# A first product over six accumulators, and no VectorE conditioning tile inside the recurrence

## The chip, the cores and the metric

The program runs on one core of a Trainium2 chip. The metric is the device time of one execution in microseconds. A core has TensorE (PE; its weight loads are PEld), VectorE (DVE), ScalarE (ACT), GpSimd (POOL) and SyncE (SP), which here only issues DMAs. Each engine works through its own queue strictly in order and waits there for what its next instruction needs.

## The reference

A decoder trunk of four layers over 256 tokens of 1024 features, float32. Each layer has a token mixer and a gated feed-forward part with a causal convolution, and both are modulated by a conditioning vector:

```
c_act = silu(c)
for i in range(4):
    sh1, sc1, g1, sh2, sc2, g2 = split(c_act @ ada_w[i] + ada_b[i], 6)      # 1024 x 6144 per layer
    h = rmsnorm(x, mix_norm_g[i]) * (1 + sc1) + sh1
    y = (gmlp, latent attention, hgrn2, gmlp)[i](h)
    x = x + (1 + g1) * y
    h = rmsnorm(x, ffn_norm_g[i]) * (1 + sc2) + sh2
    x = x + (1 + g2) * conv_ffn(h)                                          # 1024 -> 2 x 2816 -> 1024
return rmsnorm(x, final_g)
```

The gMLP mixer computes `u, v = split(gelu(h @ w_in))` with 2048 features each, normalises v over its features, mixes it over tokens, multiplies by u and projects back. The hgrn2 mixer computes q, a forget gate f, i and g from h (1024 features each), runs a gated recurrence over the tokens, normalises, gates with silu(g) and projects back.

## The kernel before

Every weight matrix comes from HBM once. A *unit* is one raw tile of 128 x 2048 float32 (1 MiB), loaded by SP into a ring of five raw buffers. Each of its halves (128 x 1024) is split into a high part by an ACT cast (`wh`, line 215) and a low part by a DVE subtraction (`wl`, line 223); a few low parts come from an ACT multiplication and an accumulating DMA of POOL instead (lines 220 and 221). There are seven `wh` and seven `wl` buffers. A product is three matmul passes: high by high, high by low, low by high. `unit()` loads and converts up to three units ahead of the one it returns, and then calls `pacing()`.

The conditioning vectors (`c_act @ ada_w`) are computed beside the products, 1 MiB of `ada_w` at a time, in two ways. Seven of the vectors go through TensorE (`ada_tensor`, line 337, in the two halves of the PSUM bank `adaps`). Fifteen go through VectorE (`ada_vector`): four tiles each, and each tile is one DMA (line 353) and two DVE operations of multiply and sum (line 362). The table `RATE` tells how many tiles a stage starts per unit, first for TensorE, then for VectorE. `pacing()` adds the rate to a counter at each unit, loads a tile when the counter reaches one, and runs it two units later; VectorE tiles start only while more than two units of the mixer or the feed-forward part are left. `need()` runs what is missing when a vector is used. The stages, in order: `mix` (the v product), `u`, `go` of the gMLP, `up` and `dn` of the feed-forward part; `lev` (the levels of the recurrence) and `hout` in layer 2.

The order of each engine's queue comes from a list scheduler that simulates the program in the order in which it is written, and lets an instruction go ahead where it expects it to be ready. `tc.issue_after` pins an instruction behind another on its engine.

The two places that the change touches first:

- **The first product (layer 0, `proj_tok_first` with `start`).** Its input needs the first two conditioning vectors, which come in eight pieces (`ada_first`, one DMA of 1 MiB and 32 small matmuls each, line 388). The string `FIRST` interleaves them: `a3` turns two blocks of x if 3 were even (line 495), computes the 3rd piece and modulates block 3 of the input (lines 395 to 398, 509, 516, 520); `v3` multiplies this block by its weights; `d` issues the next weight load; `p` issues late parameters. The product runs K-outermost: for each of the eight blocks, the 1024 first features of v are accumulated in four PSUM banks (`acc`, four buffers), 8 high matmuls (line 750) and 4 low ones (line 758) of 512 columns each. The other 1024 features come in two blocks of 512 by `proj_tok` (lines 253 to 255). The transposed blocks of x and the pieces' sums lie in the pool `misc`, three buffers of one bank.
- **The levels of the recurrence (layer 2, `hgrn`).** After the products for f and q, DVE multiplies q by k in four pieces (line 1181), and PE sums them (`sums`, line 1165); in the loop over m from 1 to 128, ACT takes exponentials (lines 1197 and 1202), DVE multiplies and adds (1198, 1200, 1203, 1207 to 1211), and PE forms the products of neighbouring pieces (`grams`, line 1156, and lines 1224 to 1239). Between them stand the product `hi` (lines 253 to 255, four units) and `hg` (lines 705 to 709, four units).

Of the kernel before, what the change touches and what calls it, by code (L numbers as in the profile page):

```python
# [18 lines left out]
D = 1024  # L19
S = 256  # L20
L = 4
P = 128
KC = D // P
EPS = 1e-6
NF = 22
GI = 2048
# [9 lines left out]
PIECES = [(0, 0, 512), (0, 512, 512), (1, 0, 512), (1, 512, 256), (1, 768, 256)]  # L36
WARM = 22
WARM2 = 5
FIRST = "a0 d v0 a1 a2 d v1 a3 v2 a4 d v3 a5 v4 a6 d v5 a7 v6 p v7"
DMA_AHEAD = 1  # L40
LAG = 2
OLAG = 1
# [4 lines left out]
HOLD = (3, 4)  # L47
ADA_P = [(1, 1), (1, 2), (1, 3), (1, 4), (2, 3), (2, 4), (3, 5)]
ADA_D = [(l, u) for l in range(L) for u in range(6) if (l, u) > (0, 1) and (l, u) not in ADA_P]
RATE = {("mix", 0): (0.05, 0.9), ("u", 0): (0.1, 0.85), ("go", 0): (0.35, 0.4), ("up", 0): (0.1, 0.2),  # L50
        ("dn", 0): (0.0, 0.4), ("mix", 1): (2.0, 0.0), ("up", 1): (0.0, 0.26), ("dn", 1): (0.0, 0.9),
        ("mix", 2): (0.0, 0.0), ("lev", 2): (0.5, 0.3), ("hout", 2): (0.25, 0.0), ("up", 2): (0.0, 0.2),
        ("dn", 2): (0.0, 0.75), ("mix", 3): (0.0, 0.5), ("u", 3): (0.0, 0.6), ("go", 3): (0.0, 0.55),
        ("up", 3): (0.0, 0.0), ("dn", 3): (0.0, 0.0)}
MAGIC = 12582912.0
TWO_PI = 2.0 * math.pi
# [35 lines left out]
def build(ctx, tc, A, out, stages=None):  # L92
# [23 lines left out]
    def acc(name, shape=(P, 512)):  # L116
        return pp.tile(list(shape), F32, tag="acc", name=name, bufs=4)

    def misc(name, shape=(P, 512)):
        return pp.tile(list(shape), F32, tag="misc", name=name, bufs=3)  # L120
# [50 lines left out]
    def want(aps, again=()):  # L171

        plan.extend((*a, i in again) for i, a in enumerate(aps))
# [6 lines left out]
    def dma_next():  # L180
        ap, n, _ = plan[state["dma"]]
        raw = wp.tile([P, 2048], F32, tag="raw", name=f"raw{state['dma']}", bufs=NRAW)
        state["dma"] += 1
        if state["dma"] == 1:

            nc.sync.dma_start(raw[:, :1024], ap[:, :1024])
            raw_, ap = raw[:, 1024:], ap[:, 1024:]
        else:
            raw_ = raw[:, :n]
        i = nc.sync.dma_start(raw_, ap)  # L190
        state["lastdma"] = getattr(i, "ins", i)
        raws.append((raw, n))
# [34 lines left out]
    def unit(ahead=None, more=DMA_AHEAD):  # L227
        u = state["use"]
        ahead = state["ahead"] if ahead is None else ahead
        while state["dma"] < min(len(plan), u + ahead + (more if u else 0)):  # L230
            dma_next()
        while state["conv"] < min(len(plan), u + ahead) or halves:
            conv_half()
        state["use"] += 1
        r = ready.pop(0)
        pacing()
        return r

    def pace(kind, l, left=None, tag=None):
        state["rate"] = dict(zip("pd", RATE[kind, l]))  # L240
        state["gap"] = GAPS[2 * l + (kind in ("up", "dn"))]
        if left is not None:
            state["left"] = left
        if tag is not None:
            state["tag"] = tag
# [126 lines left out]
    firsts = {}  # L372

    def ada_first(l, c):

        raw = wp.tile([P, KC, 4, 64], F32, tag="raw", name=f"adaf{c}", bufs=NRAW)
        rawf = raw[:].rearrange("p a b c -> p (a b c)")
        for o in (0, 1024) if c == 0 else ():
            nc.sync.dma_start(rawf[:, o : o + 1024], A["ada0"][l, c, :, o : o + 1024])
        if c:  # L380
            nc.sync.dma_start(rawf, A["ada0"][l, c])
        ps = misc(f"adaf{c}", (P, 64))
        with contextlib.ExitStack() as es:
            if "pe" in firsts:
                es.enter_context(tc.issue_after(firsts["pe"]))
            for kc in range(KC):
                for j in range(4):
                    i = pe.matmul(ps[32 * j : 32 * j + 32, :], crep(kc), raw[:, kc, j, :], start=kc == 0, stop=kc == KC - 1,
                                  tile_position=(0, 32 * j))
            firsts["pe"] = getattr(i, "ins", i)  # L390
        firsts[c] = ps

    def first_store(l, c):
        tr = t1(f"adaft{c}", 64)
        dve.transpose(tr[:], firsts[c][:])
        for e in range(2):
            b = 8 * e + c
            dve.tensor_tensor(mod[:, l, b : b + 1], tr[:, 32 * e : 32 * e + 1], prm[:, col("ada_b", l * 48 + b) : col("ada_b", l * 48 + b) + 1],
                              op=ALU.add)
        mod_post(l, 8 + c, 1)  # L400
# [329 lines left out]

    def proj_tok_first(name, sink, start=None):

        ps = [acc(f"{name}{i}") for i in range(4)]

        def chunk(kc):
            if kc % 2 == 0:
                firsts["w"] = unit(1, 0) if start else unit(2)
            with contextlib.ExitStack() as es:
                if start and kc < KC - 1:
                    es.enter_context(tc.issue_after(firsts["pe"]))  # L740
                w = firsts["w"][kc % 2]
                if not start:
                    if kc:
                        low(kc - 1, firsts["wp"])
                    firsts["wp"] = w
                for b in range(2):
                    s = slice(b * 512, b * 512 + 512)
                    for t in range(2):
                        for e in range(2):
                            i = pe.matmul(ps[2 * b + t][:], hh[:, kc, t * P : t * P + P], w[e][:, s], start=kc == 0 and e == 0, stop=False)  # L750
                if start or kc == KC - 1:
                    i = low(kc, w)
            firsts["pe"] = state["mm"] = getattr(i, "ins", i)

        def low(kc, w):
            for b in range(2):
                for t in range(2):
                    i = pe.matmul(ps[2 * b + t][:], hlo[:, kc, t * P : t * P + P], w[0][:, b * 512 : b * 512 + 512], start=False, stop=kc == KC - 1)
            return i

        if start:
            start(chunk)
        else:
            for kc in range(KC):
                chunk(kc)
        for i in range(4):
            sink(i // 2, i % 2, ps[i])

    hk = lambda k: hh[:, k, :]
# [1 line left out]


    def gmlp_units(j):
        want([(A["gmv"][j, i], 2048) for i in range(8)])
        want([(A["gmu"][j, i], 2048) for i in range(8)])
        want([(A["gmo"][j, i], 2048) for i in range(8)])

    def gmlp(l, j, start=None):
# [6 lines left out]

        proj_tok_first("v", sink, start)
        if start:
            pace("mix", l, 20)
        proj_tok(3, "v", sink, 2)

        nsh = sm("nsh", 2)
        ss = sm("ss", 8)
# [647 lines left out]
def pack(i):  # L1440
# [19 lines left out]
    def atk(W):  # L1460

        return np.ascontiguousarray(W.reshape(-1, 2, P, D).transpose(0, 2, 1, 3)).reshape(-1, P, 2048)
# [22 lines left out]
    r["pos"] = np.ascontiguousarray(np.broadcast_to(f["positions"], (P, S)))  # L1485
    wi = f["gm_w_in"]
    r["gmu"] = np.stack([bt(w, [rng(t * P, P) for t in range(16)], 2) for w in wi])
    r["gmv"] = np.stack([np.concatenate([atk(w[:, GI : GI + D]), at(w[:, GI + D :])]) for w in wi])
    r["gmo"] = np.stack([atk(w) for w in f["gm_w_out"]])
    r["gmg"] = f["gm_ln_g"]  # L1490
    r["gmbs"] = f["gm_b_s"].reshape(2, -1)
# [39 lines left out]
```

## Time and profile before

| | |
|---|---|
| median of 3 runs | 1361.19 us (1359.21 to 1361.55) |
| the profiled execution | 1361.2 us |
| its span, first to last instruction | 1359.5 us |
| PE busy | 1318.8 us (97%) |
| DVE busy | 1108.9 us (82%) |
| ACT busy | 798.4 us (59%) |
| mean granted TensorE clock | 0.992 of 2.4 GHz |
| read from HBM | 337.45 MB, 249 GB/s over the span |

A matmul of 512 columns starts every 0.23 us and one of 256 columns every 0.12 us where PE runs without a stop; the duration that the trace lists for one (0.39 and 0.28 us) includes its way through the array and overlaps the next. So a lost microsecond is seen in the distance of starts and in the idle time in square brackets, less well in the busy share.

### The profile page before, as it was taken

How to read it: one execution, taken by the hardware profiler on the slowest of the kernel's cores; microseconds unless marked ns; L12 is line 12 of the kernel's file. 1: busy time of each engine (PE TensorE's matmuls, PEld its weight loads, DVE VectorE, ACT ScalarE, POOL GpSimd, SP SyncE). 2: the span in 40 equal slices, each digit the busy share in tenths (PEclk: the TensorE clock that was granted, in tenths of full speed). 3: DMA queues.
4: the chain of work that ended last, by engine and by line, in shares of the span. 5: the costliest groups of instructions: out<-in, count | busy, mean ns of one | idle time of the engine just before them, and what ended most of it. 6: DMA issues, size and time to landing. Idle time of an engine off the chain costs nothing.

```text
span 1359.5 us, 25127 instructions
## 1 busy us (share of the span) xinstructions
PE 1318.8 (97%) x10197; PEld 1198.6 (88%) x10197; DVE 1108.9 (82%) x1847; ACT 798.4 (59%) x1248; POOL 38.0 (3%) x47
## 2 busy tenths in 40 slices
PE   8999999999999999999978899999999999999997
PEld 7799899997787899988876879999778998999986
DVE  5699889889775789899856877888988896888874
ACT  4664576665456576654675457666455754666652
POOL 0010000000000000000021000000001000000000
PEclk9999999999999999999999999999999999999999
DMA  9978975756976466599688384466978589455550
GB/s 379 356 260 317 377 261 181 273 204 267 403 263 203 127 226 248 180 350 396 223 253 242 127 306 159 164 254 257 338 282 321 193 322 375 142 171 182 202 197 31
DMA packets 51899, 340.15 MB, mean 250 GB/s; under 512 B 6852, under 2 KB 8004, under 8 KB 12998
## 3 DMA queue, kind: packets, MB, share of 16 engines
q1 hardware_dynamic: 48032, 326.95, 64.3%
q0 software_dynamic: 2592, 9.44, 3.8%
q10 hardware_dynamic: 1160, 2.17, 0.5%
q8 instruction: 80, 1.31, 0.4%
q14 instruction: 35, 0.29, 0.1%
HBM read 337.45 MB, written 1.08 MB: 249 GB/s over the span
## 4 chain that ended last, share of the span: by engine, by line
PE 72%; DVE 13%; DMA 6%; ACT 5%; issue 4%; SPq 0%; ACTq 0%; DVEq 0%
PE up L705 11%; PE up L706 11%; PE up L709 11%; PE dn L254 4%; PE dn L255 4%; PE dn L253 4%; DVE wl L223 3%; DVE adaw L362 2%; ACT wh L215 2%; DVE x L548 2%; DMA adaf<-ada 1%; PE v L750 1%; DMA adaw<-adad 1%; DVE gated L547 1%; PE up L693 1%
## 5 line engine op out<-in xcount | busy, mean ns | idle before, releaser
L215 ACT CAST wh<-raw 128x1024 fp32r<-128x1024 f32 x418 | 429.0, 1050 | 312.0 <-PE up L706 94.6
L223 DVE TENSOR_TENSOR wl<-raw,wh 128x1024 fp32r<-128x1024 f32 x400 | 485.5, 1229 | 96.8 <-ACT wh L215 96.3
L705 PE MATMUL up<-hh,wh 128*128 128x256 f32 x1280 | 314.3, 283 | 0.0
L706 PE MATMUL up<-hlo,wh 128*128 128x256 f32 x1280 | 314.1, 283 | 0.0
L705 PEld LDWEIGHTS up<-hh,wh 128*128 128x128 f32 x1280 | 245.7, 192 | 0.8 <-ACT y L1324 0.8
L706 PEld LDWEIGHTS up<-hlo,wh 128*128 128x128 f32 x1280 | 245.7, 192 | 0.0
L709 PE MATMUL up<-hh,wl 128*128 128x256 f32 x1280 | 179.7, 283 | 0.0
L709 PEld LDWEIGHTS up<-hh,wl 128*128 128x128 f32 x1280 | 165.1, 192 | 0.0
L362 DVE CUSTOM_DVE_ANT_0 adaw<-adaw,cbc,prm 128x1024 f32<-128x1024 f32 x120 | 151.2, 1276 | 11.6 <-DMA adaw<-adad 11.6
L254 PE MATMUL dn<-wl,gh 128*128 128x512 f32 x339 | 132.6, 391 | 1.3 <-DVE wl L223 1.3
L1324 ACT ACTIVATE y<-up,cwb 128x256 f32<-128x256 f32 x176 | 99.0, 562 | 58.6 <-DVE y L1326 58.6
L253 PE MATMUL dn<-wh,gh 128*128 128x512 f32 x339 | 130.3, 390 | 1.4 <-DVE y L1326 1.4
L255 PE MATMUL dn<-wh,gl 128*128 128x512 f32 x339 | 131.0, 389 | 0.0
L1325 DVE SCALAR_TENSOR_TENSOR y<-up,cwb,y 128x255 f32<-128x255 f32 x176 | 84.2, 478 | 29.1 <-ACT y L1324 28.4
L1326 DVE SCALAR_TENSOR_TENSOR y<-up,cwb,y 128x254 f32<-128x254 f32 x176 | 83.9, 477 | 1.4
L254 PEld LDWEIGHTS dn<-wl,gh 128*128 128x128 f32 x339 | 63.6, 188 | 16.4 <-DVE wl L223 3.4
L253 PEld LDWEIGHTS dn<-wh,gh 128*128 128x128 f32 x339 | 63.6, 188 | 14.9 <-issue 1.8
L255 PEld LDWEIGHTS dn<-wh,gl 128*128 128x128 f32 x339 | 63.6, 188 | 13.1
L705 PE MATMUL u<-hh,wh 128*128 128x256 f32 x256 | 64.6, 290 | 0.0
L706 PE MATMUL u<-hlo,wh 128*128 128x256 f32 x256 | 62.8, 283 | 0.0
L654 DVE TENSOR_TENSOR gl<-g,gh 128x256 fp32r<-128x256 f32 x88 | 37.0, 420 | 20.9 <-ACT gh L653 19.0
L653 ACT CAST gh<-g 128x256 fp32r<-128x256 f32 x88 | 35.3, 401 | 30.0 <-DVE g L1331 29.5
(388 smaller groups left out, 2250.9 us busy)
## 6 DMA issues: line engine op xcount, KB each, us to landing
raw<-up SPq DMA_DIRECT2D x88, 1024.0 KB
adaw<-adad SPq DMA_DIRECT2D x60, 1024.0 KB
raw<-dn SPq DMA_DIRECT2D x44, 1024.0 KB
adaw<-adap SPq DMA_DIRECT2D x28, 1024.0 KB
raw<-gmu SPq DMA_DIRECT2D x16, 1024.0 KB
raw<-gmo SPq DMA_DIRECT2D x16, 1024.0 KB
raw<-gmv SPq DMA_DIRECT2D x15, 1024.0 KB
adaf<-ada SPq DMA_DIRECT2D x7, 1024.0 KB
```

Source lines behind the costliest of these rows:

```text
L215: act.copy(wh[:, :w], raw[:, o : o + w])
L223: i = dve.tensor_tensor(wl[:, :w], raw[:, o : o + w], wh[:, :w].bitcast(F32), op=ALU.subtract)
L253: pe.matmul(ps, lh, rh, start=start, stop=False)
L254: pe.matmul(ps, lh, rl, start=False, stop=False)
L255: i = pe.matmul(ps, ll, rh, start=False, stop=stop)
L362: r = dve.tensor_tensor_reduce(raw[:, e, :], raw[:, e, :], cbc[:], 1.0, prm[:, c0 : c0 + 1], ALU.mult, ALU.add, mod[:, l, b : b + 1])
L705: pe.matmul(ps[:, g, :], a, src_h(k), start=k == 0, stop=False)
L706: pe.matmul(ps[:, g, :], a, src_l(k), start=False, stop=False)
L709: i = pe.matmul(ps[:, g, :], b, src_h(k), start=False, stop=k == nk - 1)
L1324: act.activation(y[:], ps[:, e, :], AF.Identity, bias=b, scale=w[2])
L1325: dve.scalar_tensor_tensor(y[:, 1:], ps[:, e, : S - 1], w[1], y[:, 1:], op0=ALU.mult, op1=ALU.add)
L1326: dve.scalar_tensor_tensor(y[:, 2:], ps[:, e, : S - 2], w[0], y[:, 2:], op0=ALU.mult, op1=ALU.add)
```

## The change

The first product takes 1536 features through the K-outermost loop, in six banks (four of `acc`, two of `misc`), and only the last 512 by `proj_tok`. Its weights come as eight loads of 128 x 1536 (`gmw`, 768 KiB, one per block), then two of 2048 (`gmx`), where there were eight of 2048 (`gmv`); `FIRST` has a `d` per block. The pieces of the first conditioning vectors are summed in the two halves of the bank `adaps`, no longer in `misc`. The rates of VectorE's conditioning tiles go to zero in `lev` and up in `u` and `go` of layer 0, `up` and `dn` of layer 1, and `dn` of layer 2. The second gMLP (layer 3) keeps its loop.

```diff
-FIRST = "a0 d v0 a1 a2 d v1 a3 v2 a4 d v3 a5 v4 a6 d v5 a7 v6 p v7"
+FIRST = "a0 d v0 a1 d a2 d v1 a3 d v2 a4 d v3 a5 d v4 a6 d v5 a7 d v6 p v7"
...
-RATE = {("mix", 0): (0.05, 0.9), ("u", 0): (0.1, 0.85), ("go", 0): (0.35, 0.4), ("up", 0): (0.1, 0.2),
-        ("dn", 0): (0.0, 0.4), ("mix", 1): (2.0, 0.0), ("up", 1): (0.0, 0.26), ("dn", 1): (0.0, 0.9),
-        ("mix", 2): (0.0, 0.0), ("lev", 2): (0.5, 0.3), ("hout", 2): (0.25, 0.0), ("up", 2): (0.0, 0.2),
-        ("dn", 2): (0.0, 0.75), ("mix", 3): (0.0, 0.5), ("u", 3): (0.0, 0.6), ("go", 3): (0.0, 0.55),
+RATE = {("mix", 0): (0.05, 0.9), ("u", 0): (0.1, 1.0), ("go", 0): (0.35, 0.5), ("up", 0): (0.1, 0.2),
+        ("dn", 0): (0.0, 0.4), ("mix", 1): (2.0, 0.0), ("up", 1): (0.0, 0.32), ("dn", 1): (0.0, 0.97),
+        ("mix", 2): (0.0, 0.0), ("lev", 2): (0.5, 0.0), ("hout", 2): (0.25, 0.0), ("up", 2): (0.0, 0.2),
+        ("dn", 2): (0.0, 0.87), ("mix", 3): (0.0, 0.5), ("u", 3): (0.0, 0.6), ("go", 3): (0.0, 0.55),
...
-            raw_, ap = raw[:, 1024:], ap[:, 1024:]
+            raw_, ap = raw[:, 1024:n], ap[:, 1024:]
...
-        ps = misc(f"adaf{c}", (P, 64))
+        ps = adaps[:, c % 2, :64]
...
-        ps = [acc(f"{name}{i}") for i in range(4)]
+        nb = 3 if start else 2
+        ps = [(acc if i < 4 else misc)(f"{name}{i}") for i in range(2 * nb)]
...
-            if kc % 2 == 0:
-                firsts["w"] = unit(1, 0) if start else unit(2)
+            if start:
+                firsts["w"] = unit(1, 0)
+            elif kc % 2 == 0:
+                firsts["w"] = unit(2)
...
-                for b in range(2):
-                    s = slice(b * 512, b * 512 + 512)
+                for b in range(nb):
...
-        want([(A["gmv"][j, i], 2048) for i in range(8)])
+        if j:
+            want([(A["gmv"][i], 2048) for i in range(8)])
+        else:
+            want([(A["gmw"][i], 1536) for i in range(8)])
+            want([(A["gmx"][i], 2048) for i in range(2)])
...
         if start:
-            pace("mix", l, 20)
-        proj_tok(3, "v", sink, 2)
+            pace("mix", l, 18)
+        else:
+            proj_tok(3, "v", sink, 2)
```

## Rows read from the trace of the kernel before

**Rows 1.** The page: the span, and the busy time of each engine with its share and instructions.

```profile
span 1359.5 us, 25127 instructions
PE 1318.8 (97%) x10197; PEld 1198.6 (88%) x10197; DVE 1108.9 (82%) x1847; ACT 798.4 (59%) x1248; POOL 38.0 (3%) x47
```

**Rows 2.** Two stretches in the recurrence: busy us of each engine (instructions), then the granted clock, the DMA engines' share and GB/s.

```profile
700.00:710.00 10.00, 6.83 (x50) 6.16 (x48) 2.03 (x3) 4.61 (x6) 1.73 (x2) 0.98 1.03 305
710.00:720.00 10.00, 5.08 (x16) 2.74 (x17) 6.07 (x8) 1.04 (x1) 0.00 (x0) 0.50 0.86 268
```

**Rows 3.** The timeline of DVE there: start, duration, operation, and in brackets the idle time before it and what ended it.

```profile
702.27 1.23 DVE L223 TENSOR_TENSOR wl<-raw,wh 128x1024 fp32r<-128x1024 f32 x1 [1.45 <-ACT wh L215]
711.77 1.28 DVE L362 CUSTOM_DVE_ANT_0 adaw<-adaw,cbc,prm 128x1024 f32<-128x1024 f32 x1 [8.27 <-DMA adaw<-adad]
...
712.98 1.28 DVE L362 CUSTOM_DVE_ANT_0 adaw<-adaw,cbc,prm 128x1024 f32<-128x1024 f32 x1
...
714.18 0.68 DVE L1181 TENSOR_TENSOR hsg<-hq,hk 128x512 f32<-128x512 f32 x1
```

**Rows 4.** The timeline of PE there, in the same columns.

```profile
706.45 0.39 PE L254 MATMUL hi<-wl,hh 128*128 128x512 f32 x1
714.92 1.93 PE L1165 MATMUL psum<-hsg,ones 128*32 128x512 f32 x8 [8.09 <-DVE hsg L1181]
...
717.38 0.63 PE L253 MATMUL hi<-wh,hh 128*128 128x512 f32 x1
...
719.94 0.40 PE L253 MATMUL hi<-wh,hh 128*128 128x512 f32 x1
```

**Rows 5.** The timeline of ACT: the last copy of q, and a cast for `hi` some time later.

```profile
705.03 0.59 ACT L1142 COPY hq<-hq 128x512 f32<-128x512 f32 x1
...
718.95 1.04 ACT L215 CAST wh<-raw 128x1024 fp32r<-128x1024 f32 x1 [12.37 <-PE hi L255]
```

**Rows 6.** The chain of waits that ended last, in order of time (start, duration, what): the load of the tile of rows 3.

```profile
700.13 11.50 DMA adaw<-adad
```

**Rows 7.** The timeline of DVE later in the recurrence: two of the four other conditioning operations there (the other two come one behind the other near the end of it), and one wait.

```profile
749.31 1.28 DVE L362 CUSTOM_DVE_ANT_0 adaw<-adaw,cbc,prm 128x1024 f32<-128x1024 f32 x1
...
754.39 0.73 DVE L1158 COPY_PREDICATED haa<-gmask,gram 128x512 f32<-128x512 uint8 x1 [2.66 <-PE gram L1156]
...
778.32 1.27 DVE L362 CUSTOM_DVE_ANT_0 adaw<-adaw,cbc,prm 128x1024 f32<-128x1024 f32 x1
```

**Rows 8.** The chain of waits in the same stretch; "issue" is time in which PE waited for nothing that the profile shows.

```profile
749.79 3.60 issue
...
781.15 0.97 PE hg L709 x8
...
784.04 1.92 ACT hsg L1249
```

**Rows 9.** The timeline of PE in the first product and up to the next one (u).

```profile
13.16 1.20 PE L750 MATMUL v<-wh,hh 128*128 128x512 f32 x4
...
16.11 1.10 PE L388 MATMUL adaf<-adaf,cact 128*32 128x64 f32 x64
...
18.53 1.10 PE L388 MATMUL adaf<-adaf,cact 128*32 128x64 f32 x64 [0.73 <-DMA adaf<-ada]
...
23.30 1.10 PE L388 MATMUL adaf<-adaf,cact 128*32 128x64 f32 x64 [0.71 <-DMA adaf<-ada]
...
47.93 0.50 PE L253 MATMUL v<-wh,hh 128*128 128x512 f32 x1 [1.08 <-ACT v L783]
...
51.87 0.50 PE L254 MATMUL v<-wl,hh 128*128 128x512 f32 x1 [0.43 <-DVE wl L223]
...
54.97 0.50 PE L254 MATMUL v<-wl,hh 128*128 128x512 f32 x1 [0.29 <-DVE wl L223]
...
72.51 0.68 PE L705 MATMUL u<-hh,wh 128*128 128x256 f32 x1
```

**Rows 10.** The timeline of DVE in the first product: the turning of one piece's sums, and the last reader of the second turned block.

```profile
17.27 0.25 DVE L395 STREAM_TRANSPOSE adaft<-adaf 128x64 f32<-128x64 f32 x1 [1.32 <-PE adaf L388]
...
18.61 0.54 DVE L516 TENSOR_SCALAR nt<-xt,amul,mod 128x256 f32<-128x256 f32 x1 [0.64 <-ACT hh L509]
```

**Rows 11.** The timeline of ACT at the end of the K-outermost loop: a table of activation values is loaded for the gelu.

```profile
45.90 1.28 ACT L783 ACT_TABLE_LOAD   x1
```

**Rows 12.** The timeline of DVE in layer 0: the first conditioning operation, and the 37th subtraction (16 halves of v, 16 of u, 4 of go before it).

```profile
61.36 1.28 DVE L362 CUSTOM_DVE_ANT_0 adaw<-adaw,cbc,prm 128x1024 f32<-128x1024 f32 x1
...
135.50 1.22 DVE L223 TENSOR_TENSOR wl<-raw,wh 128x1024 fp32r<-128x1024 f32 x1
```

**Rows 13.** The timeline of PE: the first matmul that reads that 37th low half.

```profile
137.23 0.39 PE L254 MATMUL go<-wl,yh 128*128 128x512 f32 x1
```

**Rows 14.** A stretch at the start of go in layer 0, columns as in rows 2.

```profile
130.00:145.00 15.00, 15.00 (x68) 12.43 (x67) 15.00 (x23) 4.17 (x5) 0.00 (x0) 1.00 0.90 316
```

**Rows 15.** Groups of instructions of DVE, all of the span: count, busy us, mean ns, idle us before.

```profile
L362 DVE CUSTOM_DVE_ANT_0 adaw<-adaw,cbc,prm 128x1024 f32<-128x1024 f32 x120 | 151.2, 1276 | 11.6 <-DMA adaw<-adad 11.6
```

**Rows 16.** The timeline of DVE in dn of layer 1, one unit: two conditioning operations and two subtractions, and the next unit's start.

```profile
620.50 1.28 DVE L362 CUSTOM_DVE_ANT_0 adaw<-adaw,cbc,prm 128x1024 f32<-128x1024 f32 x1
...
622.91 2.35 DVE L223 TENSOR_TENSOR wl<-raw,wh 128x1024 fp32r<-128x1024 f32 x2
625.19 1.28 DVE L362 CUSTOM_DVE_ANT_0 adaw<-adaw,cbc,prm 128x1024 f32<-128x1024 f32 x1
```

More of the change, by code (lines that the diff above doesn't have):

```diff
@@ L394, in first_store @@
         tr = t1(f"adaft{c}", 64)
-        dve.transpose(tr[:], firsts[c][:])
+        dve.transpose(tr[:], firsts[c])
         for e in range(2):
@@ L731, in proj_tok_first, with part @@
     def proj_tok_first(name, sink, start=None):
-        ps = [acc(f"{name}{i}") for i in range(4)]
+        nb = 3 if start else 2
+        ps = [(acc if i < 4 else misc)(f"{name}{i}") for i in range(2 * nb)]
+        def part(w, b, e):
+            return w[b // 2][e][:, b % 2 * 512 : b % 2 * 512 + 512]
         def chunk(kc):
-            if kc % 2 == 0:
-                firsts["w"] = unit(1, 0) if start else unit(2)
+            if start:
+                firsts["w"] = unit(1, 0)
+            elif kc % 2 == 0:
+                firsts["w"] = unit(2)
             with contextlib.ExitStack() as es:
@@ L740, in chunk @@
                     es.enter_context(tc.issue_after(firsts["pe"]))
-                w = firsts["w"][kc % 2]
+                w = firsts["w"] if start else firsts["w"][kc % 2 :]
                 if not start:
@@ L745, in chunk @@
                     firsts["wp"] = w
-                for b in range(2):
-                    s = slice(b * 512, b * 512 + 512)
+                for b in range(nb):
                     for t in range(2):
                         for e in range(2):
-                            i = pe.matmul(ps[2 * b + t][:], hh[:, kc, t * P : t * P + P], w[e][:, s], start=kc == 0 and e == 0, stop=False)
+                            i = pe.matmul(ps[2 * b + t][:], hh[:, kc, t * P : t * P + P], part(w, b, e), start=kc == 0 and e == 0, stop=False)
                 if start or kc == KC - 1:
@@ L755, in low @@
         def low(kc, w):
-            for b in range(2):
+            for b in range(nb):
                 for t in range(2):
-                    i = pe.matmul(ps[2 * b + t][:], hlo[:, kc, t * P : t * P + P], w[0][:, b * 512 : b * 512 + 512], start=False, stop=kc == KC - 1)
+                    i = pe.matmul(ps[2 * b + t][:], hlo[:, kc, t * P : t * P + P], part(w, b, 0), start=False, stop=kc == KC - 1)
             return i
@@ L765, in proj_tok_first @@
                 chunk(kc)
-        for i in range(4):
+        for i in range(2 * nb):
             sink(i // 2, i % 2, ps[i])
@@ L1487, in pack @@
     r["gmu"] = np.stack([bt(w, [rng(t * P, P) for t in range(16)], 2) for w in wi])
-    r["gmv"] = np.stack([np.concatenate([atk(w[:, GI : GI + D]), at(w[:, GI + D :])]) for w in wi])
+    r["gmw"], r["gmx"] = np.ascontiguousarray(wi[0][:, GI : GI + 1536].reshape(KC, P, 1536)), at(wi[0][:, GI + 1536 :])
+    r["gmv"] = np.concatenate([atk(wi[1][:, GI : GI + D]), at(wi[1][:, GI + D :])])
     r["gmo"] = np.stack([atk(w) for w in f["gm_w_out"]])
```

## The prediction

> **What bounds the kernel now.** I read the page first: PE is busy 97% of 1359.5 us [rows 1], and the change neither adds nor removes a matmul of the three passes. So it can only gain or lose where PE waits, and I went through PE's timeline for gaps, then through the stretches around them, then to DVE and ACT to see who ended each. Outside the stage changes between layers the largest gap is in the recurrence. In 700 to 720 us PE is busy 11.9 of 20 us, and in the second half the granted clock is 0.50 [rows 2], the lower of its two levels (1.2 instead of 2.4 GHz). PE has issued a `hi` matmul at 706.45 and its next instruction, the sums over q times k, starts at 714.92 after 8.09 us of idling for DVE's `hsg` [rows 4]. DVE was not working: its next instruction was a conditioning tile, for which it stood 8.27 us until the load had landed, then two operations, then `hsg` [rows 3]. The load was issued at 700.13 and took 11.50 us [rows 6]. In the first product the gaps are small: 0.73, 0.71, 1.08, 0.43 and 0.29 us [rows 9].
>
> **The change, part by part.**
>
> *How many tiles move.* I add each stage's rate unit by unit, load at one and run two units later. VectorE's tiles run, before and after: layer 0 mixer 12 and 12; up of layer 1 6 and 7; dn of layer 1 8 and 9; recurrence 3 and 0; dn of layer 2 7 and 8; u of layer 3 4 and 5, its go 5 and 4; the rest alike, 60 in all, of two operations each [rows 15]. The vectors due in layer 2's mixer end with the 36th tile, and 12 + 4 + 4 + 7 + 9 = 36 run before it, so no tile is forced into the recurrence by `need()`. A tile costs DVE two operations, of which the second starts 1.21 us after the first [rows 3], so 2.4 us.
>
> *The recurrence, removed.* The first of the three tiles goes, so DVE reaches `hsg` when its other input is there: the last copy of q ends at 705.03 + 0.59 = 705.62 [rows 5], DVE's subtraction before it at 703.5 [rows 3]. `hsg` takes about 0.65 us, so it ends near 706.3; PE is through with its `hi` matmul at 706.45 + 0.23. The sums then start at about 706.7 instead of 714.92: 8.2 us. What is late next is the copy of q, at most 0.3 us. Behind the idle stretch PE ran at half clock: the sums took 1.93 us, by the clock 0.97 of it too much, and from 717.38 to 719.94 the `hi` matmuls start every 0.43 us instead of 0.23, with the one before them seven times 0.20 = 1.4 us [rows 4]. Together 2.3 us more, and 10.5 in all. Behind that comes the rest of `hi`, for which ACT's casts wait for PE [rows 5], and the exponentials behind these casts move with them. Bounds: nothing, if another input of the sums is as late, and 10.5 + 4.8 = 15.3 if the four other operations were paid in full. Those four I cost at nothing. The one at 749.31 is followed by 2.66 us in which DVE waits for PE anyway [rows 7], and PE there stands 3.60 us for its own issue [rows 8]; that at 778.32 lies beside PE's `hg` product, which runs through to 782.1; the last two lie beside the end of ACT's silu and its squares, which the chain follows there [rows 7, 8]. A conditioning tile of TensorE moves one unit later, since its counter gets two units less in layer 0, and so into about the slot of rows 6, which landed at 711.6; PE comes to it before the last of four `hi` units, three units of 24 x 0.23 us behind 706, so near 722: nothing.
>
> *The first product.* PE has the same 192 matmuls, 18 a block instead of 12; only waits change. Block 0 takes 6 x 0.23 = 1.4 us longer, so piece 1 starts at about 17.5 instead of 16.11 and ends at 18.55. The turned blocks now have one `misc` buffer, since two hold accumulators. Blocks 2 and 3 can be turned only when the last reader of block 1 is through: before, 18.61 + 0.54 = 19.15, 1.95 us after piece 1's end at 17.21 [rows 9, 10]; so now 20.5. With 0.5 us of turning and 1.03 for piece 2, block 1's product starts at 22.1, not 19.56: 2.55 us later, 1.4 of it work moved forward, so 1.2 us lost. The later turnings have a product of 4.1 us between the reader and themselves, so nothing. The 0.71 us before piece 3 goes, 0.87 with its pipeline refill: a block now takes PE 4.1 + 1.1 us, while its 1.75 MiB take the DMA 4.2 us, since between the two starts that waited for a piece, 18.53 and 23.30, two MiB landed. The load of a block stays ahead, so the last two weight tiles land and are cast before the loop ends, which removes 0.43 and 0.29 (1.06 in distances of starts), and ACT, idle there, has its table load of 1.28 us [rows 11] behind it, and the first bank is complete five low matmuls before the end instead of three, 0.46 us sooner, so of 1.08 (1.24) I leave 0.4. Sum: -0.87 - 1.06 - 0.84 + 1.2 = -1.6 us. Bounds: -4.2, with no wait for the turned blocks, to +3, with that wait at each of three turnings (3 x 1.2) and half of the gains.
>
> The Trainium skill, PSUM — Partial Sum Buffer, section "PSUM bank collisions raise a hardware error", says that two engines must not be in one bank and quadrant at once even in different columns, so each piece's matmuls must wait for DVE's turning of the piece before, though they have halves of their own. That turning ends 0.3 us after the piece [rows 9, 10]; the only two pieces without a product between them, 1 and 2, are held longer by the turned blocks. By the rule with nothing else between, the sum would be +0.3 us; the trace of before has no such sharing.
>
> *VectorE in layer 0.* Before, two tiles ran while v was made, when DVE had room (the first at 61.36 [rows 12]); now all twelve run from u on, where DVE comes to work without a pause [rows 14]. At go's fifth K block the low half is ready at 136.7 and first used at 137.23 [rows 12, 13], so a slack of 0.5 us. Up to there one tile more stands in the queue, 2.4 us, and PE comes 1.6 us sooner; against that u's first halves can be converted before v is through, some 3 us sooner. I take +1.0; bounds 0 and 2.4 + 1.6 - 0.5 = +3.5.
>
> *The other tiles.* In dn of layer 1 a unit with a tile takes DVE 4.7 us [rows 16] and PE 24 x 0.23 = 5.5, so a tile in the one unit that had none is hidden; in up and in dn of layer 2 the spacing is wider. I take +0.5 for all; bounds 0 and three tiles unhidden, +7.2.
>
> *Sum.* The profiled execution took 1361.2 us, 1.7 us of it outside the span, which nothing here touches; the median is 1361.19. 1361.2 - 10.5 - 1.6 + 1.0 + 0.5 = 1350.6 us.
>
> **The rivals.**
>
> *The levels keep part of it (1355.6).* The gap moves to the `grams`: PE stands there for its own issue, 3.60 us in one place [rows 8], and DMAs run beside it. If it comes to these earlier and its instructions do not, half of the 10.5 is given back: 1350.6 + 5. For it: the wait has no releaser in the profile; against: it stands in the middle of the grams, which move as a block.
>
> *More is gained (1346).* The four other operations are half paid (2.4) and layer 0 costs nothing (1.0 and 0.5) with a first product at -2.5. Against: rows 8, where the chain is ACT and PE.
>
> *Slower (1364).* VectorE's queue is the bound wherever a tile is added. Place: layer 0 from u on, up and dn of layer 1, dn of layer 2. Price: 2 x 2.4 + 3 x 2.4 = 12, and 1.2 for the turned blocks, less the 10.5: +2.7. It decides where the slack of a low half is under 2.4 us; one such place shows in [rows 12, 13], and [rows 16] speak against the others.
>
> *The change does not do what it says (1361).* The scheduler puts another wait on the slot of `hsg`, a late load or a cast, and the rest cancels. Against: no second wait for a load shows there [rows 3].
>
> **How the numbers follow.** My forecast, 1350.6, has 0.64; part kept 0.16; more gained 0.10; slower 0.05; not done 0.05. The range 1346.0 to 1357.5 holds the first two and the edge of the third. A difference under 0.2%, 2.7 us, can't be told from no change here: faster is 0.64 + 0.16 + 0.10 = 0.90, same 0.05, slower 0.05.
>
> **What would show it.** In the profile after: no operation of line 362 between the products for q and the projection of layer 2; DVE's `hsg` right behind the copy of q; PE's first sums within 1 us of the `hi` matmul before them; the granted clock near 1.0 in these 20 us; the start of `grams` some 10 us sooner than the rest of the shift explains. PE idle about 2 us before the second turning, and none above 0.5 us from block 1 to the start of u, which begins near 70.9. In go of layer 0 a wait for `wl` of 1 to 2 us. I am wrong if PE waits for the sums as long as before, if waits for `wl` come up by 2 us in several stages, or if the six banks hold up block after block.

## The result and the profile after

The change makes the kernel slower: 1367.32 us median of 7 runs against 1361.80 of the kernel before on the same chip, ratio 1.0045, 95% interval 1.0031 to 1.0058. The forecast was 1350.6 us, with a range of 1346.0 to 1357.5. The profiled execution took 1369.07 us. The head of its page:

```profile
span 1367.3 us, 25166 instructions
...
PE 1323.5 (97%) x10197; PEld 1202.2 (88%) x10197; DVE 1105.1 (81%) x1851; ACT 799.6 (58%) x1252; POOL 37.7 (3%) x47
```

The gap that the prediction went for is gone. The timelines of PE and of DVE where the sums stood in [rows 3, 4]:

```profile
721.97 0.39 PE L253 MATMUL hi<-wh,hh 128*128 128x512 f32 x1
722.29 1.07 PE L1175 MATMUL psum<-hsg,ones 128*32 128x512 f32 x8
723.28 0.50 PE L254 MATMUL hi<-wl,hh 128*128 128x512 f32 x1
```

```profile
721.40 0.69 DVE L1191 TENSOR_TENSOR hsg<-hq,hk 128x512 f32<-128x512 f32 x1 [2.15 <-ACT hq L1152]
```

The sums start 0.32 us after the `hi` matmul in front of them, where [rows 4] has 8.47, and `hsg` waits for the copy of q and no longer for a load. So the loss lies elsewhere. I followed it by landmarks: the start of the same PE instruction in each trace, as a difference to the trace before (us; minus is sooner). The columns on the right belong to the experiments below.

| PE starts | before | after | first_alone | rates_alone | no_load | tiles_up0 | combo2 |
|---|---|---|---|---|---|---|---|
| u, layer 0 | 72.51 | +3.7 | +2.7 | +0.1 | +2.9 | -0.3 | -1.3 |
| go, layer 0 | 126.00 | +5.2 | +4.7 | +0.1 | +4.8 | -0.3 | -1.5 |
| second turning, layer 0 | 173.91 | +8.1 | +7.8 | -0.2 | +6.4 | -0.6 | +1.0 |
| up, layer 0 | 175.78 | +9.5 | +9.2 | -0.2 | +6.4 | -0.6 | +2.1 |
| dn, layer 1 | 590.67 | +8.7 | +9.3 | +0.2 | +6.2 | +2.8 | +5.3 |
| first turning, layer 2 | 656.72 | +13.3 | +9.8 | +3.9 | +7.8 | +4.1 | +7.4 |
| the sums | 714.92 | +7.4 | +11.4 | -2.8 | -0.5 | -3.9 | -1.0 |
| second turning, layer 2 | 822.47 | +6.5 | +12.2 | -5.9 | -2.2 | -6.5 | -3.6 |
| first turning, layer 3 | 1014.49 | +7.7 | +12.4 | -4.5 | -0.9 | -7.2 | -4.4 |

The column of after shows three losses: 5.2 us up to go of layer 0, 4.3 from there to up, and 4.6 over dn of layer 1 and its end. The recurrence gives 6.8 back. Each column is one trace, and traces differ from their start: the first matmul of v begins at 13.16 us in the kernel before, at 13.66 here, and between 12.81 and 14.11 in the others. So 0.5 of the 5.2 us stands there before the product; counted from that matmul it is 4.7 here, and 4.6 in the three other runs with the same code up to go (`first_alone`, `no_load`, `no_ops`). First the timeline of PE in the first product, with one wait in u:

```profile
19.61 1.05 PE L388 MATMUL adaps<-adaf,cact 128*32 128x64 f32 x58 [0.54 <-DVE adaft L395]
...
21.72 0.63 PE L495 MATMUL xt<-ident,gx 128*128 128x128 f32 x4 [1.05 <-DVE nt L516]
...
66.89 0.73 PE L253 MATMUL v<-wh,hh 128*128 128x512 f32 x2 [2.85 <-ACT wh L215]
...
68.16 0.74 PE L254 MATMUL v<-wl,hh 128*128 128x512 f32 x1 [0.53 <-DVE wl L223]
...
76.19 0.68 PE L705 MATMUL u<-hh,wh 128*128 128x256 f32 x1
...
83.80 1.20 PE L871 MATMUL sv<-wsp,v 128*128 128x128 f32 x8 [1.18 <-DVE wsp L851]
```

The second line is the wait for the turned block, at the place and nearly of the size that was forecast. The third is new: PE stands 2.85 us for a cast of ACT. The last line is new too: in u, PE stands 1.18 us for DVE, which has eight subtractions to do behind the late casts, to 77.91 us. What ACT did meanwhile, from its timeline (the last of six gelus, the first and last of six squares, then eight casts in one group):

```profile
60.36 0.62 ACT L792 ACTIVATE v<-v 128x512 f32<-128x512 f32 x1
...
61.56 0.72 ACT L807 ACTIVATE jk<-v,nsh 128x512 f32<-128x512 f32 x1 [0.49 <-DVE nsh L811]
...
65.11 0.71 ACT L807 ACTIVATE jk<-v,nsh 128x512 f32<-128x512 f32 x1
65.81 7.67 ACT L215 CAST wh<-raw 128x1024 fp32r<-128x1024 f32 x8
```

The weights for this cast were issued by 45.3 us; it stood behind the gelus and squares. The windows (columns as in [rows 2]) show what came with it, what goes with the two other losses, and last the stretch of the sums:

```profile
60.00:70.00 10.00, 6.63 (x25) 4.76 (x24) 3.46 (x4) 9.51 (x21) 4.84 (x3) 0.91 0.33 118
175.00:185.00 10.00, 4.95 (x47) 3.87 (x47) 8.71 (x23) 6.55 (x18) 0.00 (x0) 0.79 1.04 330
665.00:675.00 10.00, 5.80 (x40) 5.06 (x33) 8.78 (x25) 7.95 (x22) 0.13 (x1) 0.70 0.62 184
715.00:725.00 10.00, 10.00 (x73) 8.05 (x76) 6.34 (x7) 5.55 (x8) 1.72 (x2) 1.00 1.04 323
```

In 60 to 70 us ACT is the busy engine (9.51 of 10), and the DMA engines fall to 0.33, since buffers that wait for a cast can't be loaded again. In the next two PE is half idle at a granted clock of 0.79 and 0.70, part of the time on the lower level. Their gaps, on PE's timeline (the tile of PE that fills a part of the stage change, and the turning behind it):

```profile
175.00 1.93 PE L337 MATMUL adaps<-adaw,cact 128*32 128x256 f32 x32
181.99 3.65 PE L495 MATMUL xt<-ident,gx 128*128 128x128 f32 x16 [5.05 <-DVE ss L475]
...
662.98 2.80 PE L337 MATMUL adaps<-adaw,cact 128*32 128x256 f32 x48
669.97 3.71 PE L495 MATMUL xt<-ident,gx 128*128 128x128 f32 x16 [4.20 <-DVE gx L483]
```

The same two in the kernel before:

```profile
173.91 2.12 PE L495 MATMUL xt<-ident,gx 128*128 128x128 f32 x16 [2.12 <-DVE ss L475]
...
656.72 2.21 PE L495 MATMUL xt<-ident,gx 128*128 128x128 f32 x16 [1.45 <-DVE gx L483]
```

Idle time went from 2.12 to 5.05 and from 1.45 to 4.20 us, and the 16 turnings behind it take 3.7 us in place of 2.1 or 2.2. The releaser named is the end of the normalization. Where it was late, one reads on DVE's and ACT's timelines of the changed kernel ahead of it:

```profile
169.62 1.23 DVE L223 TENSOR_TENSOR wl<-raw,wh 128x1024 fp32r<-128x1024 f32 x1 [2.86 <-ACT wh L215]
172.46 1.22 DVE L223 TENSOR_TENSOR wl<-raw,wh 128x1024 fp32r<-128x1024 f32 x1 [1.61 <-ACT wh L215]
173.60 0.68 DVE L547 TENSOR_TENSOR early<-go,gx 128x512 f32<-128x512 f32 x1
```

```profile
163.28 2.01 ACT L215 CAST wh<-raw 128x1024 fp32r<-128x1024 f32 x2 [2.85 <-DMA raw<-gmo]
166.64 1.05 ACT L215 CAST wh<-raw 128x1024 fp32r<-128x1024 f32 x1 [1.35 <-DMA raw<-up]
```

The same step of DVE in the kernel before:

```profile
160.57 1.23 DVE L223 TENSOR_TENSOR wl<-raw,wh 128x1024 fp32r<-128x1024 f32 x1 [2.06 <-ACT wh L215]
164.38 1.22 DVE L223 TENSOR_TENSOR wl<-raw,wh 128x1024 fp32r<-128x1024 f32 x1 [2.58 <-ACT wh L215]
165.53 0.68 DVE L547 TENSOR_TENSOR early<-go,gx 128x512 f32<-128x512 f32 x1
```

In both kernels DVE is idle (4.5 us in all in the changed one, 4.6 before) and only then comes to `early`, the first step of the residual. What changed is when: `early` starts 8.1 us later, though go began only 5.2 us later. In its queue the subtractions of the next stage's first weights stand ahead of the residual; these wait for ACT's casts, and the casts for loads. The loads are late because a tile comes later in the queue (layer 0 still has twelve), as SP's queue shows, first in the changed kernel, then before:

```profile
153.26 0.33 SPq L353 DMA_DIRECT2D adaw<-adad  x1
155.68 0.33 SPq L190 DMA_DIRECT2D raw<-gmo  x1
159.44 5.21 SPq L190 DMA_DIRECT2D raw<-up  x3
```

```profile
143.17 0.33 SPq L353 DMA_DIRECT2D adaw<-adad  x1
145.58 2.60 SPq L190 DMA_DIRECT2D raw<-gmo  x2
151.20 5.21 SPq L190 DMA_DIRECT2D raw<-up  x3
```

A tile is issued at 153.26, ahead of go's last weights, where before the last tile goes at 143.17, with two of go's loads still behind it in place of one; the loads for up begin 8.2 us later. The DMA engines are busy without a pause from 150 to 180 us (shares 1.01, 1.00 and 1.03; before 1.01, 1.04 and 0.98), and a stretch full of such loads (630 to 640 us) moves 428 GB/s, so that 1 MiB takes 2.45 us. At the end of dn of layer 1 the last tile stands right ahead of the first weights of layer 2 in both kernels (627.70 and 628.12 us before, 642.98 and 643.36 after), but with a ninth tile in dn these weights are issued 15.2 us later than before, where dn began 8.7 us later.

### The profile page after: what moved, and what is told of

Same layout as the page of the kernel before. It is cut to its first block, busy times and chain, and to the rows that moved or that the text cites. A ratio compares the mean times of both kernels' runs of the same rounds, so it can differ in the third digit from the quotient of the medians.

```text
span 1367.3 us, 25166 instructions
## 1 busy us (share of the span) xinstructions
PE 1323.5 (97%) x10197; PEld 1202.2 (88%) x10197; DVE 1105.1 (81%) x1851; ACT 799.6 (58%) x1252; POOL 37.7 (3%) x47
## 5 line engine op out<-in xcount | busy, mean ns | idle before, releaser
L215 ACT CAST wh<-raw 128x1024 fp32r<-128x1024 f32 (+1 forms) x422 | 429.4, 1041 | 323.7 <-PE up L706 89.3
L223 DVE TENSOR_TENSOR wl<-raw,wh 128x1024 fp32r<-128x1024 f32 (+1 forms) x404 | 483.5, 1213 | 105.8 <-ACT wh L215 105.3
L253 PEld LDWEIGHTS dn<-wh,gh 128*128 128x128 f32 x339 | 63.7, 188 | 15.2 <-ACT warm L630 1.7
```

What stands on the lines that cost most here:

```text
L215: act.copy(wh[:, :w], raw[:, o : o + w])
L223: i = dve.tensor_tensor(wl[:, :w], raw[:, o : o + w], wh[:, :w].bitcast(F32), op=ALU.subtract)
L253: pe.matmul(ps, lh, rh, start=start, stop=False)
```

## The experiments

The idle times that the expectations name are up to 0.4 us longer than the rows have them in brackets (5.42 for 5.05, 4.57 for 4.20).

**The two halves of the change apart.** `first_alone` has the new first product and layer 0's rates, `rates_alone` the rest.

```
first_alone = after with:  ("up", 1): 0.26, ("dn", 1): 0.9, ("lev", 2): 0.3, ("dn", 2): 0.75
rates_alone = before with: ("up", 1): 0.32, ("dn", 1): 0.97, ("lev", 2): 0.0, ("dn", 2): 0.87
```

> The first product on six banks with layer 0's new rates; the rates of up and dn of layer 1, of the recurrence and of dn of layer 2 as before, so three conditioning tiles of VectorE run in the recurrence again. In the changed kernel TensorE's landmarks lie 3.7 us later than before at the start of u, 8.1 us at layer 0's second normalization, 10.3 at the start of layer 1's mixer and 8.7 in the middle of it. Theory A (the loss of this part is made in layer 0, by ACT's order and by loads that come late): the shift is there again, nothing gives it back, and the idle time before the sums in the recurrence is back at some 8 us: 1361.4 + 8 = 1369 to 1371. Theory B (VectorE's queue wherever a tile is added): layer 0 has no tile more in all, so at most 2 us are lost: 1361 to 1364.

> The first product and layer 0's rates as before; up and dn of layer 1, the recurrence and dn of layer 2 with the new rates, so no conditioning tile of VectorE runs in the recurrence. In the changed kernel the shift against before grows by 4.5 us over dn of layer 1 and its end, falls by 6.8 over the recurrence and grows by 1.3 over dn of layer 2. If the parts add up: 1361.4 - 1 = 1360.5, with the 4.5 us standing again where dn of layer 1 ends (PE's gap there above 4 us, 1.82 before). If that gap came only from what layer 0 had shifted: 1361.4 - 6 = 1355. My forecast for these parts was -10.5 + 0.5, 1351.

`first_alone`: 1371.38 us, ratio 1.0071 (1.0056 to 1.0086). `rates_alone`: 1358.95, ratio 0.9982 (0.9972 to 0.9992). The differences, +10.2 and -2.3 us against 1361.22, add up to +7.9, somewhat more than the 5.5 of the whole change, which was timed with other runs of the kernel before. In `first_alone` PE's wait for the sums is back, and in `rates_alone` the gap at the end of dn of layer 1 stands by itself, without anything late from layer 0:

```profile
726.36 1.93 PE L1175 MATMUL psum<-hsg,ones 128*32 128x512 f32 x8 [8.08 <-DVE hsg L1191]
```

```profile
660.63 3.71 PE L495 MATMUL xt<-ident,gx 128*128 128x128 f32 x16 [3.40 <-DVE gx L483]
```

From that turning to layer 2's second one `rates_alone` gains 3.9 + 5.9 = 9.8 us: nearly the 10.5 that were forecast for the recurrence. It pays 3.7 of them ahead of it, over dn of layer 1 and its end.

**The load or the operations.** Two of the added tiles, once without their load, once with operations of 8 columns.

```
no_load:
+            n = 4 * ADA_D.index((l, u)) + i
+            if n not in (11, 35):
                 nc.sync.dma_start(raw[:]..., A["adad"][n // 4, i])
...
+                        src = cbc[:] if n in (11, 35) else raw[:, e, :]
no_ops:
+                        w = 8 if n in (11, 35) else D
+                        r = dve.tensor_tensor_reduce(raw[:, e, :w], raw[:, e, :w], cbc[:, :w], ...
```

> The changed kernel, but two of VectorE's conditioning tiles, the last that go of layer 0 loads (the 12th) and the last that dn of layer 1 loads (the 36th), are not loaded: their two operations of 1024 columns each run at the same places on the silu of the condition instead, so the conditioning vectors of these tiles are left wrong. Theory A (the price of the added tile is its load of 1 MiB, which pushes the first weights of the next stage back, and these are converted ahead of the residual): PE's gap at layer 0's end falls from 5.42 to about 2.5 us and that at the end of dn of layer 1 from 4.57 to about 1.8 us, and the half clock behind each goes with it: 2.7 to 4.3 us each, 1367.3 - 7 = 1360 (1358 to 1362). Theory B (the price is two operations on VectorE, 2.4 us): both gaps as in the changed kernel, 1367.

> The changed kernel, but the operations of the same two tiles (the 12th and the 36th) work on 8 columns of 1024, so that VectorE has 2.2 us less for each while both are loaded as before; the conditioning vectors of these tiles are left wrong. Theory A (the load): both gaps as in the changed kernel, 5.4 and 4.6 us, 1366 to 1367.5. Theory B (VectorE): gaps of 2.5 and 1.8 us, 1360.

`no_load`: 1360.33 us, ratio 0.9997 (0.9983 to 1.0011). `no_ops`: 1366.55, ratio 1.0044 (1.0027 to 1.0061), as the changed kernel. The two turnings of `no_load`, and those of `no_ops`:

```profile
180.34 2.12 PE L498 MATMUL xt<-ident,gx 128*128 128x128 f32 x16 [2.46 <-DVE ss L478]
...
664.55 2.21 PE L498 MATMUL xt<-ident,gx 128*128 128x128 f32 x16 [1.33 <-DVE gx L486]
```

```profile
180.43 3.54 PE L497 MATMUL xt<-ident,gx 128*128 128x128 f32 x16 [3.96 <-DVE ss L477]
...
668.20 3.71 PE L497 MATMUL xt<-ident,gx 128*128 128x128 f32 x16 [3.34 <-DVE gx L485]
```

Two loads of 1 MiB are worth the whole 7 us (6.5 by the ratios). A tile takes a buffer too (in layer 0's mixer one of the five raw ones); `no_load` leaves it that and its operations, so what it takes away is the transfer. Without the two loads the idle times fall to 2.46 and 1.33 us, the turnings run at full clock, and the recurrence gives 10.0 us (from +7.8 to -2.2) in place of 6.8. The operations of VectorE are worth some 1 us of idle time at each place, and the half clock stays. From go to up of layer 0, 4.3 us are lost in the changed kernel, 1.6 in `no_load` and 3.3 in `no_ops`; over dn of layer 1 and its end 4.6, 1.7 and 3.7.

**ACT's order.** Two more units are converted at the last block, ahead of the squares.

```
-                firsts["w"] = unit(1, 0)
+                firsts["w"] = unit(3 if kc == KC - 1 else 1, 0)
```

> The changed kernel with one edit: at the eighth block of the first product the weights of two more units are converted, so that the casts for the last 512 features come ahead of the six squares in ACT's queue. Theory A (ACT's order: PE stands 2.85 us for a cast behind six squares, the raw buffers stay full and the loads pause from 60 to 70 us, which makes the first loads of up late at layer 0's end): the wait goes, u starts 3 to 5 us sooner, the loads go on in 60 to 70 us, and the gap at layer 0's end (5.42 us) falls back to about 2.5: 1367.3 - 4 to - 7, 1360 to 1363. If layer 0's end hangs on the tile that was moved to go alone, only the first part comes: 1363 to 1365. Theory B (VectorE's queue): no change, 1367, since VectorE was idle there.

1369.07 us, ratio 1.0052 (1.0038 to 1.0067): no gain, a miss for Theory A's time. Its first half holds: the wait for the cast is gone and PE begins u 1.9 us before the kernel before does. Then it stops in u for the sums of the spatial weights:

```profile
72.84 3.34 PE L830 MATMUL rsum<-ws,ones 128*128 128x512 f32 x4 [1.83 <-POOL ws L826]
...
183.42 3.65 PE L495 MATMUL xt<-ident,gx 128*128 128x128 f32 x16 [5.37 <-DVE ss L475]
```

The load of `ws` is issued from ACT's queue, among the squares. And layer 0's end waits 5.37 us, no less than before the edit. Whether the pause of the loads has a part in that isn't shown, since the edit only moved it: the share of the DMA engines is 0.64 in place of 0.33 in 60 to 70 us, but 0.50 in place of 0.89 in 70 to 80 us.

**The recurrence's tiles in up of layer 0**, with the first product of before:

```
-("up", 0): (0.1, 0.2)    ("lev", 2): (0.5, 0.3)
+("up", 0): (0.1, 0.34)   ("lev", 2): (0.5, 0.0)
```

> The kernel before with the recurrence's rate at 0 and the three tiles run in up of layer 0 instead, where the DMA engines are busy 30 to 70% of the time and the last operand tile is ready some us ahead of PE. Theory A (what an added tile costs is its load of 1 MiB where the loads stand one behind the other, in go of layer 0 and dn of layer 1): nothing is lost here and the recurrence gives its 7 to 10 us: 1351 to 1355. Theory B (two operations of 1.2 us on VectorE wherever a tile is added, 7.2 us for three): 1358 to 1361.

1354.33 us, ratio 0.9952 (0.9936 to 0.9968): faster than both kernels. But Theory A's "nothing is lost here" is wrong: dn of layer 0 and its end lose 3.5 us (from -0.6 to +2.8), and the first units of dn wait for VectorE's subtractions, 0.55 and 2.43 us, where before one wait of 1.36 us stands:

```profile
311.14 0.50 PE L254 MATMUL dn<-wl,gh 128*128 128x512 f32 x1 [2.43 <-DVE wl L223]
```

The recurrence pays for it with 10.6 us. `early_tiles` puts the same three tiles further forward (up of layer 0 at 0.36, its dn at 0.3, up of layer 1 at 0.28):

> The kernel tiles_up0 with the same three tiles earlier: up of layer 0 at 0.36, its dn at 0.3 and up of layer 1 at 0.28, so that eight tiles run inside up of layer 0 and three in its dn. In tiles_up0 TensorE lost 3.5 us against before from the end of up of layer 0 (waits of 0.72 and 2.59 us in the first units of dn, a gap of 3.11 us at its end), where two tiles ran right at the change from up to dn. Theory A (place decides: VectorE and the loads have room inside up and none at its end): these waits fall back to those of before and 1 to 3 us are gained: 1351.5 to 1353.5. Theory B (a tile costs its two operations wherever it is put): 1354.3 as tiles_up0.

1355.24 us, ratio 0.9951 (0.9931 to 0.9970), the same within the intervals. From up to the end of dn of layer 0 it loses 3.1 us (from +1.4 to +4.5), with four waits for `wl` of 0.4 to 1.4 us in dn. Theory A's forecast missed here; a tile in up costs something at the start of dn in both places that I tried. The +1.4 stands before any of these tiles runs: at layer 0's end, with the code of `tiles_up0` up to there, the turnings fell to half clock behind 1.95 us of idling, where `tiles_up0` kept full clock behind 1.81.

```profile
173.88 3.62 PE L495 MATMUL xt<-ident,gx 128*128 128x128 f32 x16 [1.95 <-DVE ss L475]
```

**The new first product mended.** `combo` has the casts early, the small loads ahead of the squares, and layer 0's tiles loaded early; `combo2` the rates of before in u and go.

```
combo:   casts as above; squares emitted behind the loads of Gb, ws and bs; pace("mix", l, 19) from step "p" on;
         ("mix", 0): 1.0, ("u", 0): 1.11, ("go", 0): 0.15, and the other rates of tiles_up0
combo2:  ("mix", 0): 1.2, ("u", 0): 0.85, ("go", 0): 0.4, and the other rates of early_tiles
```

> The new first product with the weights of two more units converted at its last block, the three small loads of the gMLP issued ahead of the squares, and layer 0's twelve tiles loaded as early as can be (three by the end of v, eight in u, one in go); the recurrence's three tiles in up of layer 0, and up and dn of layer 1 and dn of layer 2 at the rates of before. It differs from the kernel tiles_up0 in the first product and in where layer 0's tiles stand. Theory A: the first product is 1.5 to 2 us faster once its casts are in time and layer 0's end is as before: 1354.3 - 2 = 1352 (1351 to 1354). Theory C (the six banks gather ACT's work, six gelus, six squares and the casts, into the one stretch that is left of v, and what is taken from one wait comes back at the sums for u): u is through as late as in the changed kernel or 1 to 2 us less, some 3 to 5 us behind before, and the time is 1357 to 1359.

> The kernel combo with layer 0's rates of before in u and go (three tiles loaded by the end of v, seven in u, two in go) and the other rates of early_tiles. In combo TensorE left u 0.8 us ahead of before and then lost 4.4 us by layer 0's end, with waits of 3.45, 1.21 and 0.75 us for VectorE in go, where four operations of two tiles stood in one piece in its queue. Theory A (the new first product is worth 0.5 to 2 us once ACT's order is mended, and the loss behind it was the tiles' place): the waits in go are gone, and the time is early_tiles less 0.5 to 2 us, 1350 to 1353. Theory C (the new first product gives nothing that layer 0 does not take back): the time of early_tiles or 1 to 4 us more.

`combo`: 1358.35 us, ratio 0.9976 (0.9961 to 0.9991). `combo2`: 1356.13, ratio 0.9964 (0.9951 to 0.9977). In both PE leaves u ahead of the kernel before, by 0.8 and 1.5 us; counted from the first matmul of v by 1.1 us each, and by 0.9 in `combo2_no_load` below, which has the same code up to there. So the six banks do give some two thirds of the 1.6 us that were forecast once the casts and the small loads are in time, against Theory C. But the total is no better than without them, as Theory C had it, since go and layer 0's end take it back:

```profile
140.77 0.50 PE L254 MATMUL go<-wl,yh 128*128 128x512 f32 x1 [3.29 <-DVE wl L223]
```

```profile
137.65 0.50 PE L254 MATMUL go<-wl,yh 128*128 128x512 f32 x1 [1.06 <-DVE wl L223]
...
174.93 3.32 PE L495 MATMUL xt<-ident,gx 128*128 128x128 f32 x16 [3.26 <-DVE ss L475]
```

The first line is `combo`, where the operations of two tiles stood close together in VectorE's queue; the others are `combo2`: PE came sooner, waited 1.06 us in go and 3.26 us at layer 0's end. Two runs asked whether go's loads hold that end.

> The kernel combo2, but layer 0's last conditioning tile of VectorE before its second normalization (the 12th) is not loaded; its two operations work on the silu of the condition, so the conditioning vector of this tile is left wrong. In combo2 TensorE left u 1.5 us ahead of before and stood 1.22 us in go and 3.64 us at layer 0's end, where the DMA engines are busy all the time. Theory D (the loads of go set when layer 0 ends, whatever TensorE has gained before): without 1 MiB in that stretch the gap falls to 2 to 2.5 us and layer 0's second normalization begins 1.2 to 2.5 us sooner than in combo2, that is before the kernel before does: 1353.5 to 1355. Theory E (the gap is made by VectorE's queue): gap and time as in combo2, 1356.

> The kernel early_tiles, which has the first product of before, with the same 12th tile not loaded (its conditioning vector is left wrong). It shows what the load costs where TensorE comes to layer 0's end later. Theory D: TensorE's gap there is 2.3 us already, near the 2.1 us that the chain from the last product to the normalization needs, so at most 0.5 us is gained, and the new first product shows its 1.2 to 2 us between these two kernels: early_no_load 1354.5 to 1355.5, some 1 to 2 us above combo2_no_load. Theory E: as early_tiles, and no lower than combo2_no_load.

`early_no_load`: 1353.87 us, ratio 0.9931 (0.9916 to 0.9947); `combo2_no_load`: 1357.00, ratio 0.9944 (0.9921 to 0.9967). With the first product of before, PE's idle time at layer 0's end fell to 0.53 us, below the 2.1 that I had taken for the least:

```profile
172.04 1.95 PE L498 MATMUL xt<-ident,gx 128*128 128x128 f32 x16 [0.53 <-DVE ss L478]
```

In `combo2_no_load` it stayed at 2.78. There the loads for up began only at 154.34, 6.4 us after go's last one and right behind two subtractions of DVE that end at 154.31 and free a raw buffer, so the missing load freed little: from go to up 2.4 us are lost in place of 3.6. Theory D's forecasts missed: `combo2_no_load` is slower than the 1353.5 to 1355 that it gave, with a gap above its 2 to 2.5 us, and `early_no_load` is faster than its 1354.5 and than `combo2_no_load`, with a gap 1.4 us shorter than the 1.95 of `early_tiles`, where it allowed 0.5. Both times overlap in their intervals with those without the edit. What the new first product is worth with a free end of layer 0 stays open.

## Why the prediction was wrong

*The recurrence (-10.5 us): right.* 9.8 to 10.6 us in `rates_alone`, `no_load` and `tiles_up0`. The sums follow the `hi` matmul by 0.32 us, the granted clock there is 1.00, and the slot that shows it is `hsg` behind the copy of q, as forecast. In the changed kernel itself it came to 6.8. Up to the sums, where 8.2 were forecast, it gained 5.9 us, with a granted clock of 0.71 in the 10 us from the first turning on; `rates_alone` and `no_ops` gained 6.8 and 6.9 there (0.83), `tiles_up0` and `no_load` 7.9 and 8.4 (1.00). So with the half clock behind the longer gap go 2 to 2.5 us of it here. Behind the sums, where 2.3 were forecast, it gained 0.9, and 1.6 to 3.9 in those four. The rival of the levels, half of the gain given back before the grams, didn't come in them; in the changed kernel the gaps before the grams keep 6.1 us, of 6.9 before and 3.3 to 5.3 in those four, and so may hold the rest of what is missing (last section).

*The first product (-1.6 us): +5.2 at go in this kernel, 4.7 of them its own.* The wait for the turned block came (1.05 us), the waits from block 1 to the end of the loop went, that for ACT's table load too, and the sharing of a bank by the pieces' sums shows as one wait of 0.54 us for DVE's turning: the rule of the Trainium skill's page PSUM — Partial Sum Buffer that was weighed (section "PSUM bank collisions raise a hardware error") fits that row, though no run here separates it from the two halves being one tile of the program. The step that failed is "the last two weight tiles land and are cast before the loop ends", with "ACT, idle there": the second of these tiles was issued by 45.3 us but cast at 65.81, behind six gelus and six squares, and the sum had no term for ACT's queue behind the loop. The six banks put these and eight casts into the time of the one block that is left of v, where two blocks were left before. PE's 2.85, 0.53 and 1.18 us and the lower clock behind the first follow. With ACT's order mended the product gains 0.9 to 1.1 us, about two thirds of the forecast.

*VectorE in layer 0 (+1.0) and the other tiles (+0.5): +4.3 and about +5.8.* These are the steps that decided, and this is the step that failed in both: the terms were worked out from VectorE's operations, 2.4 us a tile, against its slack, as a wait for `wl` in go and as hidden units in dn. In go no wait of PE came to 0.25 us; the loss is made at the stages' ends. The tile's load was put at nothing: 1 MiB in a queue without a gap, ahead of the weights whose conversion stands ahead of the residual. It is worth 2.7 of the 4.3 and 2.9 of the 4.6 us (by `no_load`), the operations some 1 us in each (by `no_ops`). Layer 0 went past its upper bound of +3.5; the 7.2 held. The 5.8 are 4.6 over dn of layer 1 and its end and 1.2 over dn of layer 2; in up of layer 1 nothing was lost.

*The rival "slower" (1364) had the sign and the wrong reason.* It made VectorE's queue the bound wherever a tile is added; `no_ops` takes these operations away from the two places and stays at 1366.55 us, `no_load` takes the loads and gains 7 us. VectorE's queue does decide elsewhere, as at the start of dn of layer 0 in `tiles_up0` and in go in `combo`.

## What to carry to other kernels

Cost moved work by its transfer as well as by its operations: look at the DMA share of the stage that receives it, and at what stands behind the transfer in the queue. At the end of a stage, follow an in-order engine's queue forward: a conversion for the next stage that stands ahead of the last step of this one turns a late load into idle time of TensorE. And a product that is made faster by finishing more at once leaves less time for what its results set off.

## What was not expected of the hardware

An idle time at a stage change can cost more than its length here, since half clock may follow it. At the stage changes of all 13 traces, idle times of 2.68 us and more before the turnings were each followed by half clock for a part or the whole of the 16 turnings (2.63 to 3.71 us), and those of 1.62 us and less by full clock (1.94 to 2.21). Between them it went either way: 2.06 us in the changed kernel and 2.46 in `no_load` by full clock, 1.95 in `early_tiles` and 2.02 in `rates_alone` by half. So the full clock behind the 2.46 us of `no_load` may in part be luck.

The gaps before the grams that the profile calls "issue" ([rows 8] has one of 3.60 us) don't have one length: 3.30 and 3.60 us before, 4.90 and 1.19 in the changed kernel, 3.02 and 0.32 in `rates_alone`, one of 4.07 in `no_ops`. The record of the DMA packets bears on them: in each of these seven, and in every other such gap of the 13 traces, PE goes on 1.2 to 1.6 us after a packet of 16 KiB in the queue that the page lists as q8, instruction, has been moved; before, such packets start at 743.33 and 751.01 us and take 0.97 and 0.89 us, and the gaps end at 745.74 and 753.39. So PE most likely waits there for its own instructions to be loaded, and then work that comes sooner only waits longer. No run changed the instructions, so this isn't shown by experiment.
